# Keys and rotary queries turned by VectorE and DMA instead of TensorE, in the second sweep of a hybrid encoder layer

## The chip, the cores and the metric

The kernel runs on one core of a Trainium2 chip. The metric is the device time of one execution in microseconds (us); the median of several runs is given. Every stage works in float32, and most products are made of three matmuls on operands split into a high and a low part (names ending in `_h` and `_l`).

## The reference

One layer of an encoder over 2048 tokens of width 1024. One input projection feeds two groups: a gated linear attention with four heads, scanned forward and backward (group A), and a latent attention with four heads (group B). The outputs are joined, projected, and added to the residual with a layer norm. What the change touches is group B:

```python
def mla_branch(c_q, c_kv, k_rope, gate, positions, q_norm_g, w_uq, kv_norm_g, w_ukv):
    q = (rms_norm(c_q, q_norm_g) @ w_uq).reshape(B, S, 4, 128 + 64)
    kv = (rms_norm(c_kv, kv_norm_g) @ w_ukv).reshape(B, S, 4, 128 + 128)
    q_nope, q_rope = q[..., :128] * scale, apply_rope(q[..., 128:], positions) * scale
    k_nope, v = kv[..., :128], kv[..., 128:]
    k_r = apply_rope(k_rope, positions)
    ...   # for each block of 128 queries, over all 2048 keys:
    s = einsum('bqhd,bkhd->bhqk', qn, k_nope) + einsum('bqhr,bkr->bhqk', qr, k_r)
    o = einsum('bhqk,bkhv->bqhv', softmax(s), v)
    return o * silu(gate)
```

The kernel absorbs the key part of `w_ukv` into the queries, so that the normed latent `c_kv` (width 128) serves as key and as value for all heads, beside the rotary key of width 64.

## The kernel before

The tokens lie in 16 chunks of 128. The kernel has four stages one after the other.

1. **First sweep** (to about 338 us, with `late_gates` to about 349): group A's projections and scans, chunk by chunk in `sweep_a`. Its pieces are the functions `ga_...`. For most chunks, queries and keys are turned (tokens from partitions to columns) by VectorE's 32x32 stream transpose, four stores to DRAM and two loads (`turn`, `turned`). `ga_q` and `ga_k` make `qd` and `kd`, queries and keys with their decay; `ga_kt` turns `kd`.
2. **Second sweep** (`sweep_c`, 349 to about 583 us): 8 steps of two chunks. A step computes for its 256 tokens the gate of group B (`pz`, 96 matmuls in 8 parts), and for each chunk the projection `ipm` in four parts (`ipa` to `ipd`), from it the normed latents `cq` and `ckv` and the rotary key (`krf`, `krs`), the values `vh` and `vl`, and group A's last products `Ob` with its norm and gate (`oib`, `sqO`, `ss`, `rg...`, `og`, `oT`). `tm` turns `cq` (two transposes), `ckv` and `krs` (one each) on TensorE into PSUM, from which ScalarE and VectorE take `cqT_h/l`, `ckvT_h/l` and the turned `krs`. `pqr` projects the rotary queries, `qrf` rotates them, `tq` turns them by two transposes on TensorE, `qrTh/qrTl` split them, and `c_sqr` stores them (`rh_s`, `rl_s`). `pq` makes the absorbed queries `qah/qal`, stored by `c_sqa`.
3. **Attention** (to about 1080 us): 16 blocks of one head and 512 queries, each against all keys. `fetch(i)` loads the queries of block `i` into the buffers that held `pz`'s weights (`wz`); blocks 0 and 1 are fetched ahead of the loop.
4. **Output projection**, norm and store.

The order of all work in the second sweep is written by hand. `PLACE_C` gives each piece a place (step number plus a fraction, one for each chunk of the step where there are two); `PLACE_C_FIRST` and `PLACE_C_LAST` replace it in the first and the last step. `sweep_c` sorts all pieces by place and issues them in that order, and `in_order` chains the instructions of each engine, so that no engine overtakes:

```python
for _, _, fn, a in sorted(todo, key=lambda e: e[:2]):
    with self.in_order(last):
        fn(*a)
```

Nearly all DMAs are issued by SyncE (SP) from one queue in program order: a DMA that waits for its data or its buffer holds up those behind it. These are the loads of a chunk (`xcf`, the input; `SU`, `qdb`, `oib`, `ub`, group A's intermediate results) and the stores (`oa_s` from `oT`, `gm_s`, `qh_s`, `ql_s`, `rh_s`, `rl_s`). Matmul outputs lie in PSUM buffers of the tags `gp` (`pz`, `pq`, `Ob`), `ip` and `tr` (`tm`, `tq`, `pqr`).

Of the kernel before, what the change touches and what calls it, by code (L numbers as in the profile page):

```python
# [18 lines left out]
P = 128  # L19
# [4 lines left out]
H = 4  # L24
# [112 lines left out]
    "krsh", "krsl", "vh", "vl", "tm", "cqTh", "cqTl", "ckvTh", "ckvTl", "krT", "pqr", "qrf", "qrfa",  # L137
# [3 lines left out]
FETCH_C = ("lx", "xh", "xl")  # L141


PLACE_C = dict(
    ipa=(-0.08, 0.695),
# [6 lines left out]
    tq=(1.06, 1.482),  # L152
# [12 lines left out]
    qrTh=(1.16, 1.587),  # L165
# [11 lines left out]
    qrTl=(1.25, 1.687),  # L177
# [40 lines left out]
PLACE_C_FIRST = dict(  # L218
    ipa=(-1.874, 0.381),
# [6 lines left out]
    tq=(1.11, 1.512),  # L226
# [56 lines left out]
    Ob=(0.0, 0.299),  # L283
    tm=(0.495, 1.083),
    pqr=(0.749, 1.284),
    tq=(0.919, 2.161),
    xh=(-0.262, -0.109),
    sqO=(0.15, 0.374),
# [12 lines left out]
    oib=(0.063, 0.366),  # L301
# [23 lines left out]
    soT=(1.09, 2.304),  # L325
# [21 lines left out]
class K:  # L347
    def __init__(self, tc, ins, out):
        self.tc, self.nc, self.ins, self.out = tc, tc.nc, ins, out
        self.ulate = []  # L350
        self.parts = {}
# [141 lines left out]
    def run(self):  # L493
        tc, nc, ins = self.tc, self.nc, self.ins
        with ExitStack() as top:
# [8 lines left out]
            self.qr_s = [[dp.tile([H, 64, QB], F32, name=f"r{p}_s{b}") for p in "hl"] for b in range(NQB)]  # L504
            self.gm_s = [dp.tile([P, H, QB], F32, name=f"gm_s{b}") for b in range(NQB)]
            self.oa_s = [dp.tile([P, H, P], F32, name=f"oa_s{c}") for c in range(NCH)]
# [106 lines left out]
    def sweep_a(self):  # L613
        tc, nc, ins, cp = self.tc, self.nc, self.ins, self.cp
        with ExitStack() as ctx:
# [135 lines left out]
            run("k", i)  # L751
            run("q", i)
# [11 lines left out]
    def products(self, d, g, after=lambda g, k: None):  # L764
# [366 lines left out]
    def sweep_c(self):  # L1131


        with ExitStack() as ctx:
# [9 lines left out]
            def put(n, st, fn, *a, j=None):  # L1144
                last = st == len(steps) - 1
                p = PLACE_C[n]
                p = (last and PLACE_C_LAST.get(n)) or (not st and PLACE_C_FIRST.get(n)) or p
                todo.append((st + (p if j is None else p[j]), len(todo), fn, a))
# [3 lines left out]
            for s in steps:  # L1152
                for n in range(8):
                    put("pz", s["st"], self.c_pz, s, n, j=n)
                for n in STEP_C:
                    put(n, s["st"], getattr(self, "c_" + n), s)
            for d in chunks:
                for n in range(4):
                    put("ip" + "abcd"[n], d["st"], self.c_ip, d, n, j=d["j"])
                for n in CHUNK_C:  # L1160
                    if (d["st"] or n not in FETCH_C) and (d["c"] < NCH - 1 or n not in ("Sf1", "Sf2")):
                        put(n, d["st"], getattr(self, "c_" + n), d, j=d["j"])
            last = dict(self.tail)
# [42 lines left out]
    def scale_w(self, ct):  # L1206
        wa = self.w1.tile([P, H, P], F32, tag=f"qrT{'hl'[ct]}", name=f"wabs{ct}")
# [75 lines left out]
    def c_sqr(self, s):  # L1283
        b, qs = self.of_step(s)
        for t, dst in zip(s["qrT"], self.qr_s[b]):
            for pr in range(2):
                self.nc.sync.dma_start(dst[2 * pr:2 * pr + 2, :, qs].rearrange("h d t -> (h d) t"),
                                       t[:, pr].rearrange("p a t -> p (a t)").bitcast(F32))
# [57 lines left out]
    def c_krsh(self, d):  # L1346
        d["krs"] = self.w1.tile([P, 2, 64], F32R, tag="krs", name=f"krs{d['c']}")
# [10 lines left out]

    def c_tm(self, d):
        tp = d["tm"] = self.tr.tile([P, 4, P], F32, tag="tr", name=f"tm{d['c']}")  # L1360
        for i, src in enumerate((d["cq"][:, 0:P], d["cq"][:, P:2 * P], d["ckv"],
                                 d["krs"].rearrange("p a d -> p (a d)").bitcast(F32))):
            self.nc.tensor.transpose(tp[:, i], src, self.ident)
# [36 lines left out]
    def c_tq(self, d):  # L1400
        tq = d["tq"] = self.tr.tile([P, 4, P], F32, tag="tr", name=f"tq{d['c']}")
        for pr in range(2):
            self.nc.tensor.transpose(tq[:, pr], d["qr"][:, 2 * pr:2 * pr + 2].rearrange("p h d -> p (h d)"), self.ident)

    def c_qrTh(self, d):
        s = d["step"]
        if "qrT" not in s:
            s["qrT"] = [self.w1.tile([P, 2, 2, P], F32R, tag=f"qrT{p}", name=f"qrT{p}{d['st']}") for p in "hl"]
        self.hi(s["qrT"][0][:, :, d["j"]], d["tq"][:, 0:2])

    def c_qrTl(self, d):
        qrT, j = d["step"]["qrT"], d["j"]
        self.lo(qrT[1][:, :, j], d["tq"][:, 0:2], qrT[0][:, :, j])
# [106 lines left out]

    def attention(self):
# [4 lines left out]
        with ExitStack() as ctx:  # L1526
# [10 lines left out]
            def fetch(i):  # L1537
                h, b = blocks[i]
                q = stt[i]["q"] = []
                for p, src in zip("hl", self.qa_s[b]):  # L1540
                    q.append(qp.tile([P, QB], F32R, tag="wz", name=f"q{p}{i}"))
                    nc.sync.dma_start(q[-1].bitcast(F32), src[:, h])
                for p, src in zip("hl", self.qr_s[b]):
                    q.append(qp.tile([P, QB], F32R, tag="wz", name=f"r{p}{i}"))
                    for r in (slice(0, 64), slice(64, 128)):
                        nc.sync.dma_start(q[-1][r].bitcast(F32), src[h])

            def scores(i, j):
# [3 lines left out]
                qh, ql, rh, rl = d["q"]  # L1552
# [162 lines left out]
            fetch(0)  # L1715
            fetch(1)
# [22 lines left out]
            for i in range(nb):  # L1739
# [10 lines left out]
                if i + 2 < nb:  # L1750
                    put(NP * i + 4.05, fetch, i + 2)
# [300 lines left out]
```

## Time and profile before

| | |
|---|---|
| median of three runs | 1272.35 us (1271.3 to 1274.25) |
| the profiled execution | 1272.24 us, span 1270.3 us, mean granted clock 0.998 |
| TensorE, VectorE, ScalarE, GpSimd busy | 98%, 71%, 57%, 57% of the span |
| second sweep | some 349 to 583 us, steps of some 28.5 us |

The profile is of one execution. Its times count from the start of the span. PE is TensorE's matmul, PEld its weight load, DVE VectorE, ACT ScalarE, POOL GpSimd, SP SyncE with its DMA queue (SPq). A row of the timeline or the chain begins with start and duration; in brackets stands the idle time of the engine before it and what ended that. A row of a group has the line of the code, the engine, the operation, output and input tiles with shapes, the count, busy time, mean ns of one, and idle time before.

### The profile page before, as it was taken

Reading aid. Unit: us, or ns where it says so; the run is one execution under the profiler, and the core shown is the slowest. Engines: PE = TensorE matmul, PEld = TensorE weight load, DVE = VectorE, ACT = ScalarE, POOL = GpSimd, SP = SyncE. Lnnn points to the kernel's source line nnn. Section 1 sums busy time; section 2 is a strip of 40 time slices with the busy share of each in tenths; the row PEclk is TensorE's granted clock in tenths of the full one; section 3 lists DMA queues with packets and bytes.
Section 4 is the critical chain, followed back from the end, with each engine's and each line's share of the span. In section 5 each row is a group of like instructions: output and inputs, shape, how many; then the busy total and the mean of one; then the engine's idle time right before and its main releaser. Section 6 shows DMA issues by size and latency. Waiting matters only on the chain.

```text
span 1270.3 us, 19649 instructions
## 1 busy us (share of the span) xinstructions
PE 1246.8 (98%) x6946; PEld 1098.9 (87%) x6946; DVE 896.3 (71%) x1611; ACT 727.5 (57%) x1176; POOL 718.9 (57%) x443
## 2 busy tenths in 40 slices
PE   8999999999999999999999999999999999999997
PEld 7999999999799999988788888888888888887886
DVE  6635555553665555564888888888888888389997
ACT  7544343454565445454778888888888888411110
POOL 0132323223265555430798888889999999935541
PEclk9999999999999999999999999999999999999999
DMA  8224656566857766757212111201133110376652
GB/s 293 79 81 125 136 143 139 143 134 159 276 178 201 218 198 193 215 144 210 53 30 53 40 46 42 59 9 59 58 92 92 42 42 26 124 226 200 205 191 100
DMA packets 189794, 160.49 MB, mean 126 GB/s; under 512 B 98326, under 2 KB 140958, under 8 KB 189696
## 3 DMA queue, kind: packets, MB, share of 16 engines
q1 hardware_dynamic: 181632, 157.11, 43.4%
q0 software_dynamic: 672, 2.10, 0.4%
q8 instruction: 55, 0.90, 0.3%
q10 hardware_dynamic: 7392, 0.03, 0.3%
q14 instruction: 43, 0.35, 0.1%
HBM read 103.05 MB, written 56.13 MB: 125 GB/s over the span
## 4 chain that ended last, share of the span: by engine, by line
PE 68%; DVE 2%; ACT 1%; DMA 1%; issue 1%; POOL 0%; SPq 0%; DVEq 0%; POOLq 0%; ACTq 0%
PE pz L1239 7%; PE ipm L1310 5%; PE o L411 5%; PE o L413 5%; PE o L412 5%; PE pS L1556 4%; PE pS L1557 4%; PE pS L1558 4%; PE pS L1559 4%; PE pS L1560 4%; PE po L413 2%; PE po L411 2%; PE po L412 2%; PE Ob L1457 1%; PE pmb L413 1%
## 5 line engine op out<-in xcount | busy, mean ns | idle before, releaser
L363 POOL TENSOR_TENSOR pl<-s,ph 128x1024 fp32r<-128x1024 f32 x128 | 306.7, 2414 | 53.3 <-ACT ph L357 49.5
L1578 DVE TENSOR_TENSOR rm<-pS,rm 128x512 f32<-128x512 f32 x210 | 144.8, 690 | 36.4 <-ACT s L1565 30.8
L1565 ACT ACTIVATE s<-pS 128x1024 f32<-128x1024 f32 x128 | 131.3, 1025 | 61.2 <-PE pS L1560 50.8
L1602 DVE TENSOR_TENSOR s<-s,mb 128x1024 f32<-128x1024 f32 x128 | 151.2, 1213 | 8.9 <-PE mb L1596 8.2
L357 ACT ACTIVATE ph<-s 128x1024 fp32r<-128x1024 f32 x128 | 135.0, 1056 | 17.2 <-PE o L413 16.7
L1606 ACT ACTIVATE s<-s 128x1024 f32<-128x1024 f32 x128 | 131.4, 1049 | 10.6 <-DVE s L1602 10.5
L411 PE MATMUL ipa<-wah,xah 128*128 128x384 f32 (+1 forms) x384 | 129.1, 336 | 5.3 <-ACT wah L357 5.3
L412 PE MATMUL ipa<-wal,xah 128*128 128x384 f32 (+1 forms) x384 | 124.8, 325 | 0.0
L413 PE MATMUL ipa<-wah,xal 128*128 128x384 f32 (+1 forms) x384 | 124.7, 325 | 0.0
L1076 POOL TENSOR_TENSOR Sb<-Sb,Us 64x512 f32<-64x512 f32 x15 | 19.9, 1325 | 170.1 <-DVE Us L1068 161.0
L1556 PE MATMUL pS<-qh,ckvT_h 128*128 128x512 f32 x256 | 102.6, 401 | 0.8 <-DVE rm L1578 0.4
L411 PE MATMUL o<-ph,vh 128*128 128x512 f32 x256 | 101.1, 395 | 0.0
L1557 PE MATMUL pS<-ql,ckvT_h 128*128 128x512 f32 x256 | 100.0, 391 | 0.0
L1559 PE MATMUL pS<-rh,krs 128*128 128x512 f32 x256 | 100.0, 390 | 0.0
L1558 PE MATMUL pS<-qh,ckvT_l 128*128 128x512 f32 x256 | 99.9, 390 | 0.0
L1560 PE MATMUL pS<-rl,krs 128*128 128x512 f32 x256 | 99.8, 390 | 0.0
L413 PE MATMUL o<-ph,vl 128*128 128x512 f32 x256 | 99.8, 390 | 0.0
L412 PE MATMUL o<-pl,vh 128*128 128x512 f32 x256 | 99.7, 389 | 0.0
L1629 DVE TENSOR_TENSOR ap<-ap,s 128x512 f32<-128x512 f32 x120 | 83.0, 692 | 2.7 <-ACT s L1606 0.7
L411 PEld LDWEIGHTS ipa<-wah,xah 128*128 128x128 f32 x384 | 73.2, 191 | 8.5 <-ACT wah L357 5.6
L363 POOL TENSOR_TENSOR ol<-of,oh 128x512 fp32r<-128x512 f32 x32 | 43.0, 1345 | 64.6 <-ACT oh L357 63.1
L412 PEld LDWEIGHTS ipa<-wal,xah 128*128 128x128 f32 x384 | 73.2, 191 | 1.0 <-DVE wal L363 0.4
(302 smaller groups left out, 3426.0 us busy)
## 6 DMA issues: line engine op xcount, KB each, us to landing
xcf<-xT_dram SPq DMA_DIRECT2D x16, 512.0 KB, 5.6
xr<-x_dram SPq DMA_DIRECT2D x16, 512.0 KB, 6.6
out_dram<-rr SPq DMA_DIRECT2D x32, 256.0 KB, 2.1
xaf<-xT_dram SPq DMA_DIRECT2D x14, 512.0 KB, 4.2
oib<-oi_s SPq DMA_DIRECT2D x16, 256.0 KB, 4.4
qdb<-qd_s SPq DMA_DIRECT2D x16, 256.0 KB, 3.3
SU<-su_s SPq DMA_DIRECT2D x16, 256.0 KB, 3.7
ub<-u_s SPq DMA_DIRECT2D x16, 256.0 KB, 3.9
```

Source lines behind the costliest of these rows:

```text
L357: return nc.scalar.activation(dst, src, AF.Copy).ins
L363: return e.tensor_tensor(dst, src, hi.bitcast(F32), ALU.subtract).ins
L411: mm(out, ah, bh, start=start, stop=False)
L412: mm(out, ah, bl, start=False, stop=False)
L413: mm(out, al, bh, start=False, stop=stop)
L1556: mm(ps[:, e], kh, qh, start=True, stop=False)
L1557: mm(ps[:, e], kh, ql, start=False, stop=False)
L1558: mm(ps[:, e], kl, qh, start=False, stop=False)
L1559: mm(ps[:, e], kr, rh, start=False, stop=False)
L1560: mm(ps[:, e], kr, rl, start=False, stop=True)
L1578: V.tensor_tensor(d["rm"], src[:, e], d["rm"], ALU.max)
L1602: V.tensor_tensor(s, s, d["mb"][:, None, :].to_broadcast([P, 2, QB]), ALU.subtract)
```

## The change

- For chunks 0 to 13, `ckv` and `krs` are no longer turned by `tm`. A new piece `kvx` turns `vh`, `vl` and `krs` of a chunk in 32x32 blocks on VectorE (three stream transposes), `skv` stores a step's result in four DMAs to DRAM (`kv_s`), and `kv_load` loads it back, in four DMAs, into one tile `kvT` that takes the place of `ckvT_h`, `ckvT_l` and the turned `krs`. The two chunks of the last step keep the transposes on TensorE.
- `tq` becomes one stream transpose of 128x256 on VectorE into SBUF (`qrx`); `qrTh/qrTl` read that; `c_sqr` stores in eight DMAs (runs of 128 bytes) instead of four; `fetch` reads each block's rotary queries in eight DMAs of 32 partitions instead of four of 64.
- `fetch` of blocks 0 and 1 becomes part of the second sweep's order (places 8.23 and 9.35), ahead of the last stores; the rotary queries' store of step 6 and the `oT` stores of chunk 14 get later places.
- In the last step chunk 15's `Ob` (with `oib` and `sqO`) goes from place 0.299 to 0.425, which on TensorE is from behind chunk 13's `tm` to just ahead of step 6's `pq`, and `tq`, `qrTh`, `qrTl` get slightly other places.
- The last chunk of the first sweep turns its keys by four TensorE transposes and a copy instead of stream transpose, stores and loads, and `kd` is made ahead of `qd`.
- As a result of the issue order, `qal` of the last step comes on VectorE behind block 0's first maxima, just ahead of `mc`.

The core of the diff (the remaining hunks shift places of pieces named above by a few hundredths):

```diff
+LAST_C = ("ckvTh", "ckvTl", "krT")
+KV_LOADS = tuple((2 * s - 4, 2 * s - 2, float(s)) for s in range(2, NCH // 2)) + ((12, 14, 8.27),)
+LATE_STORE = {("sqr", 6): 2.31}
 PLACE_C = dict(
+    skv=1.65,
+    kvx=(1.02, 1.44),
...
-    tq=(1.06, 1.482),
+    tq=(1.13, 1.56),
 PLACE_C_LAST = dict(
...
-    Ob=(0.0, 0.299),
+    Ob=(0.0, 0.425),
...
-    soT=(1.09, 2.304),
+    soT=(1.29, 2.304),
@@ run
-            self.ckvT_h = rp.tile([P, NKT, P], F32R, name="ckvT_h")
-            self.ckvT_l = rp.tile([P, NKT, P], F32R, name="ckvT_l")
-            self.kr = rp.tile([P, NKT, P], F32R, name="krs")
+            self.kvT = rp.tile([P, NKT, 3, P], F32R, name="kvT")
+            self.ckvT_h, self.ckvT_l, self.kr = (self.kvT[:, :, i] for i in range(3))
@@ sweep_a
-            run("k", i)
-            run("q", i)
+            with self.in_order(last):
+                run("k", i)
+                run("q", i)
@@ products
-            for n in ((("lr", "qx"), ("ql", "kx", "v1"), ("kl", "v3")) if i else (("lr",), ("q2", "k2", "v1"), ("v3",)))[g]:
+            for n in ((("lr", "qx"), ("ql", "k2", "v1"), ("v3",)) if i == NCH - 1 else
+                      (("lr", "qx"), ("ql", "kx", "v1"), ("kl", "v3")) if i else (("lr",), ("q2", "k2", "v1"), ("v3",)))[g]:
@@ sweep_c
+            for a, b, place in KV_LOADS:
+                todo.append((place, len(todo), self.kv_load, (slice(a, b),)))
+            for i, place in enumerate((8.23, 9.35)):
+                todo.append((place, len(todo), self.fetch, (i,)))
@@ c_sqr
-        for t, dst in zip(s["qrT"], self.qr_s[b]):
-            for pr in range(2):
-                self.nc.sync.dma_start(dst[2 * pr:2 * pr + 2, :, qs].rearrange("h d t -> (h d) t"),
-                                       t[:, pr].rearrange("p a t -> p (a t)").bitcast(F32))
+        dst = self.qr_s[b].rearrange("r p h a (c e t) -> e r (p h a) c t", c=4, e=4)
+        for j in range(2):
+            t = s["qrT"][:, j].rearrange("p a (m t) -> p (a m) t", t=32).bitcast(F32)
+            for e in range(4):
+                self.nc.sync.dma_start(dst[e, :, :, qs.start // P + j], t[32 * e:32 * e + 32])
+    def c_kvx(self, d):
+        s = d["step"]
+        if "kvx" not in s:
+            s["kvx"] = self.w1.tile([P, 2, 3, P], F32, tag="kvx", name=f"kvx{d['st']}")
+        for i, src in enumerate((self.vh[:, d["c"]], self.vl[:, d["c"]], d["krs"].rearrange("p a d -> p (a d)"))):
+            self.nc.vector.transpose(s["kvx"][:, d["j"], i], src.bitcast(F32))
+    def c_skv(self, s):
+        t = s["kvx"].rearrange("p a i (m t) -> p (a i m) t", m=4)
+        c = 2 * s["st"]
+        dst = self.kv_s[:, c:c + 2].rearrange("r a i m (b t) -> b r (a i m) t", b=4)
+        for b in range(4):
+            self.nc.sync.dma_start(dst[b], t[32 * b:32 * b + 32])
+    def kv_load(self, cs):
+        for m in range(4):
+            self.nc.sync.dma_start(self.kvT[32 * m:32 * m + 32, cs].rearrange("p c i t -> p (c i) t").bitcast(F32),
+                                   self.kv_s[:, cs, :, m].rearrange("r c i t -> r (c i) t"))
@@ c_tm
-        for i, src in enumerate((d["cq"][:, 0:P], d["cq"][:, P:2 * P], d["ckv"],
-                                 d["krs"].rearrange("p a d -> p (a d)").bitcast(F32))):
-            self.nc.tensor.transpose(tp[:, i], src, self.ident)
+        src = (d["cq"][:, 0:P], d["cq"][:, P:2 * P])
+        if d["st"] == NCH // 2 - 1:
+            src += d["ckv"], d["krs"].rearrange("p a d -> p (a d)").bitcast(F32)
+        for i, e in enumerate(src):
+            self.nc.tensor.transpose(tp[:, i], e, self.ident)
@@ c_tq
-        tq = d["tq"] = self.tr.tile([P, 4, P], F32, tag="tr", name=f"tq{d['c']}")
-        for pr in range(2):
-            self.nc.tensor.transpose(tq[:, pr], d["qr"][:, 2 * pr:2 * pr + 2].rearrange("p h d -> p (h d)"), self.ident)
+        d["tq"] = self.w1.tile([P, 256], F32, tag="qrx", name=f"qrx{d['c']}")
+        self.nc.vector.transpose(d["tq"], d["qr"].rearrange("p h d -> p (h d)"))
@@ fetch (a method now)
+        for n, p in enumerate("hl"):
+            q.append(qp.tile([P, QB], F32R, tag="wz", name=f"r{p}{i}"))
+            for r in range(4):
+                nc.sync.dma_start(q[-1][32 * r:32 * r + 32].bitcast(F32), self.qr_s[b][:, n, h, r % 2])
@@ attention
-            fetch(0)
-            fetch(1)
```

More of the change, by code (lines that the diff above doesn't have):

```diff
@@ L218 @@
 PLACE_C_FIRST = dict(
+    skv=1.66,
+    kvx=(0.95, 1.5),
     ipa=(-1.874, 0.381),
@@ L1146, in put @@
                 p = PLACE_C[n]
-                p = (last and PLACE_C_LAST.get(n)) or (not st and PLACE_C_FIRST.get(n)) or p
+                p = (last and PLACE_C_LAST.get(n)) or (not st and PLACE_C_FIRST.get(n)) or LATE_STORE.get((n, st)) or p
                 todo.append((st + (p if j is None else p[j]), len(todo), fn, a))
```

56 lines of the change are left out of this document (31 added, 25 removed).

## The prediction

> **What bounds the kernel now.** I read the page first: its engine totals and the chain that ended last.
>
> ```profile
> span 1270.3 us, 19649 instructions
> PE 1246.8 (98%) x6946; PEld 1098.9 (87%) x6946; DVE 896.3 (71%) x1611; ACT 727.5 (57%) x1176; POOL 718.9 (57%) x443
> PE 68%; DVE 2%; ACT 1%; DMA 1%; issue 1%; POOL 0%; SPq 0%; DVEq 0%; POOLq 0%; ACTq 0%
> ```
>
> TensorE (PE) is idle for 23.5 us of the span, and the chain runs along it. Work taken off PE is time, as long as nothing else becomes late. Where that can happen is told by the table of busy time by stage (first the stretch, its length and PE's busy time; later DVE, ACT, POOL, clock, DMA share, GB/s), over the end of the first sweep, one step of the second sweep, its last step in two parts, and the start of attention.
>
> ```profile
> 320.00:338.00 18.00, 15.78 (x102) 13.47 (x101) 11.92 (x18) 7.37 (x15) 7.49 (x9) 1.00 0.75 241
> 338.00:349.00 11.00, 11.00 (x54) 9.22 (x53) 8.10 (x13) 9.34 (x17) 1.68 (x3) 1.00 1.04 381
> 448.00:477.00 29.00, 29.00 (x215) 28.26 (x214) 15.48 (x56) 14.56 (x41) 14.59 (x17) 1.00 0.71 200
> 534.00:566.00 32.00, 29.24 (x190) 26.73 (x190) 18.01 (x65) 16.37 (x46) 9.25 (x11) 1.00 0.56 149
> 590.00:620.00 30.00, 27.17 (x121) 21.49 (x120) 24.39 (x31) 19.62 (x22) 7.39 (x4) 1.00 0.65 179
> ```
>
> In a middle step PE never stops, DVE is half idle, and the DMA engines are 71% busy. So the second sweep up to about 534 us is bound by PE alone. In the last step (from 534) PE already waits 2.8 us, and 2.8 us again at the start of attention. The clock is granted in full throughout, so it plays no part.
>
> **The transposes taken off PE.** The chain of waits shows what one costs there.
>
> ```profile
> 536.50 0.44 PE tm L1363 x4
> 536.93 2.88 PE pz L1239 x24
> 574.87 0.22 PE tq L1403 x2
> ```
>
> Four in 0.44 us and two in 0.22: 0.11 us each in PE's stream. Removed are 2 of every chunk's 4 `tm` for 14 chunks (28) and all `tq` (32): 60 x 0.11 = 6.6 us at most. By my count 50 of them lie ahead of chunk 13's `Ob`, where PE is never idle; 6 lie in the stretch of the last step where PE waits anyway (below), and 4 are the `tq` of the two last chunks. I count 54 x 0.11 = 5.9 us. [...]
>
> **What DVE gets.** The change adds three 128x128 stream transposes a chunk (`kvx`) and one of 128x256 (`qrx`), and takes away one `ckvT_l`. The nearest rows are:
>
> ```profile
> L814 DVE STREAM_TRANSPOSE qx<-ipa 128x256 f32<-128x256 f32 x1 | 0.4, 440 | 0.0
> L1486 DVE STREAM_TRANSPOSE oT<-og 128x512 f32<-128x512 f32 x16 | 11.4, 711 | 0.5
> L363 DVE TENSOR_TENSOR ckvT_l<-tm,ckvT_h 128x128 fp32r<-128x128 f32 x16 | 4.6, 285 | 12.0 <-ACT ckvT_h L357 12.0
> ```
>
> A line through 440 and 711 gives 0.30 for 128 columns (bounds 0.18, a quarter of 711, and 0.44). A step of two chunks then gets 2 x (0.9 + 0.44 - 0.28) = 2.1 us: DVE 17.6 of some 28, still no bound by its total. But it works in order, and one place has little room: `og` of the second chunk frees a PSUM buffer that the next step's first `pz` writes.
>
> ```profile
> 464.78 1.13 DVE L1480 SCALAR_TENSOR_TENSOR og<-Ob,rg_r,ub 128x128 f32<-128x128 f32 x4
> 466.80 0.37 PE L1239 MATMUL pz<-xch,wzh 128*128 128x256 f32 x1
> ```
>
> `og` ends at 465.91, 0.9 us ahead of `pz`. PE will be there 0.44 earlier (two `tq`, two `tm`), and three `kvx` (0.9) come ahead of this `og` on DVE, of which DVE's short waits for ACT inside that chain swallow some half. So 0 to 0.4 us a step is lost, at most 2.4 in six steps; I take 0.1 a step, 0.6. ACT loses two copies a chunk and has only less to do.
>
> **What the queue and the DMA engines get.** Per step four stores `kv_s`, four loads `kvT` and four more stores of rotary queries are added, all on SyncE's queue, which issues in order.
>
> ```profile
> L1492 SPq DMA_DIRECT2D oa_s<-oT x52: 573/630/1139, 404.4 to 574.2; - x52
> SPq L1418 <- PE Ob L1457: 54.6, 9, 10.6
> 451.48 1.13 SPq L477 DMA_DIRECT2D xcf<-xT_dram  x1
> 460.83 1.05 ACT L357 ACTIVATE xch<-xcf 128x1024 fp32r<-128x1024 f32 x1
> xcf<-xT_dram SPq DMA_DIRECT2D x2, 512.0 KB, 5.6
> ```
>
> `oa_s` has the form of the new stores, 512 runs of 128 bytes: 0.63 us of issue. Twelve more are 7.6 us a step, and SyncE sits some 55 us of the sweep in its waits for `Ob` alone, about 7 a step; it becomes full, but not over-full. Most exposed is `xcf`, which comes behind the four `kv_s`: issued at 451.48, landed 5.6 later at 457.1, needed by ACT at 460.83, 3.7 us of room; 0.44 goes to the earlier PE and 4 x 0.63 = 2.5 to the stores, which leaves 0.8. I count nothing; the price if the cover goes is a rival below. What the added packets cost the DMA engines is bounded by two stretches:
>
> ```profile
> DMA packets 7828, 5.81 MB, mean 200 GB/s; under 512 B 4496, under 2 KB 6544, under 8 KB 7824
> DMA packets 2155, 4.19 MB, mean 381 GB/s; under 512 B 414, under 2 KB 542, under 8 KB 2155
> ```
>
> The second (338 to 349, DMA share 1.04) moves a megabyte in 11 x 16 x 1.04 / 4.19 = 43.7 us of engine time. At that price the bytes of the first (448 to 477) explain 254 of its 0.71 x 16 x 29 = 329 us; the other 75, over 4,496 packets under 512 B, are 17 ns a packet. A step gets 7,168 more such packets in place of 512 of a kilobyte, 768 of 512 bytes, and 0.79 MB more: by bytes alone 34 us (share 0.78), with 17 ns on each of 7,400 net 160 us, which is 1.05. I take the middle, 0.92: no wait on PE.
>
> **The end of the first sweep.** The last chunk's keys no longer go to DRAM and back, `kd` runs ahead of `qd`, and PE gets four transposes.
>
> ```profile
> 328.72 1.40 DVE L991 SCALAR_TENSOR_TENSOR qd<-q,E 128x512 f32<-128x512 f32 x1 [1.10 <-ACT E L974]
> 330.04 2.04 DVE L1005 TENSOR_TENSOR kd<-k,E 128x512 f32<-128x512 f32 x1
> 332.13 0.66 PE L1027 MATMUL kt<-ident,kd 128*128 128x128 f32 x4 [1.65 <-DVE kd L1005]
> ```
>
> `kd` started at 328.72 ends by 330.8 even at its 2.04 us, so PE's 1.65 us goes; the four new transposes cost 0.44 to 0.66. Gain 1.0 (bounds 0, if `qd` is now what PE waits for, and 1.2).
>
> **The last step, where I see the loss.** `oib` of chunk 14 is already the last thing DVE waits for, and behind it on DVE stands everything up to the second half of `pz`.
>
> ```profile
> 546.29 0.32 SPq L1418 DMA_DIRECT2D qdb<-qd_s  x1
> 547.18 0.86 SPq L1287 DMA_DIRECT2D rh_s<-qrTh  x2
> 548.13 0.97 SPq L1287 DMA_DIRECT2D rl_s<-qrTl  x2
> 549.15 0.92 SPq L1418 DMA_DIRECT2D oib<-oi_s  x2
> 553.52 0.70 DVE L1460 TENSOR_TENSOR Ob<-Ob,oib 128x512 f32<-128x512 f32 x1 [3.82 <-DMA oib<-oi_s]
> 566.70 0.71 DVE L1486 STREAM_TRANSPOSE oT<-og 128x512 f32<-128x512 f32 x1
> 566.72 4.56 PE pz L1239 x36
> ```
>
> The list of waits has, for the same stretch, PE's longest one:
>
> ```profile
> PE Ob L1457 <- DVE og L1480: 2.1, 1, 2.1
> ```
>
> `qdb` waits for PE's `Ob` of chunk 13, so all behind it is tied to PE. After it come four stores (1.97 us) and `oib`; in the changed order eight stores stand there, 8 x 0.63 = 5.0 us, so `oib` lands 3.1 us later. From 553.5 to 566.7 DVE works almost without a gap, and gets in this stretch three `kvx` of chunk 13 (0.9) and one `qrx` (0.44), less one `ckvT_l` (0.28): `pz` starts 3.1 + 1.1 = 4.2 us later against `Ob` 13. Bounds: 0, if the stores are issued while SyncE would have waited anyway, and 5.3 with `kvx` at 0.44 and the load slower among the stores. Moving `Ob` 15 further back on PE spares PE these 2.1 us there, but that only moves the wait, since `pz` needs the same DVE chain. I take 4.2.
>
> **The start of attention.**
>
> ```profile
> 578.49 0.54 SPq L1542 DMA_DIRECT2D qh<-qh_s  x1
> 602.69 0.39 PE L1556 MATMUL pS<-qh,ckvT_h 128*128 128x512 f32 x1
> 605.25 0.66 PE L1584 MATMUL mx<-ident,rm 128*128 128x128 f32 x4 [1.27 <-DVE rm L1578]
> 605.95 0.69 DVE L1589 TENSOR_REDUCE mc<-mx 128x4 f32<-128x512 f32 x1 [0.75 <-PE mx L1584]
> 567.34 1.19 DVE L363 TENSOR_TENSOR qal<-pq,qah 128x1024 fp32r<-128x1024 f32 x1
> ```
>
> The last `qal` now runs just ahead of `mc`: 1.19 us where DVE had 0.75 free, so block 0's maximum comes 0.45 later, with PE waiting. I add 0.25 for the loads: 0.7 (bounds 0 and 3). The second block's queries stand behind four `kvT`, eight stores of `oT`, eight of rotary queries and `gm`: with their own ten, 31 issues of 0.6 behind the first block's, some 18.6 us. From about 581 that is 599.6, and with 5 to land 604.6; the first use is at 602.69, plus the 4.2 that PE is late by then. So it just holds.
>
> **Sum:** against the profiled execution's 1272.24 (0.1 under the median of the runs): -5.9 -1.0 +0.6 +4.2 +0.7 = -1.4, so 1270.8 us. Its own range is 1268 to 1273. About 0.2%, 2.5 us, is what a measurement of this kernel tells from no change, so the forecast lies within that, near its edge.
>
> **Rival 1, the last step absorbs it.** If the eight stores go out under SyncE's wait, or the DVE chain has slack that the waits do not show, the 4.2 goes and the 6 transposes there count: 1270.8 - 4.2 - 0.7 = 1265.9; the second block's queries, then 1.9 us late, take some back: 1266 to 1268. For it speaks that PE's 2.1 us for `og` stand ahead of `Ob` 15, whose move avoids them; against it that `oib` is the releaser now.
>
> **Rival 2, slower: `xcf` late in every step.** Its cover of 0.8 us means that it may take 6.4 us to land. In the crowded stretch 320 to 338, at a DMA share of 0.75, it took
>
> ```profile
> xcf<-xT_dram SPq DMA_DIRECT2D x1, 512.0 KB, 9.3
> ```
>
> At 9.3 each of six steps loses 2.9; halfway, 7.9, it loses 1.5: 6 x 1.5 = 9, so 1279.8. It decides from 6.4 us on. For it speaks the DMA share going to 0.92; against it that at 0.71 the load takes 5.6.
>
> **Rival 3, small packets saturate the DMA engines.** At the upper bound of 1.05 a step lasts 29 x 1.05 = 30.5 us instead of PE's 29 - 0.9 = 28.1: six steps lose 14, so 1285. [...]
>
> **Rival 4, the change doesn't shorten PE:** each step's stall takes the transposes' place and only the 1.0 and the last step's loss remain: 1274 to 1276.
>
> **Chances.** Forecast 0.43, rival 1 0.30, rival 2 0.15, rival 3 0.05, rival 4 0.07. Below 1269.8 lie rival 1 and about two fifths of the forecast: 0.47. Above 1274.9 lie rivals 2 and 3, half of 4 and a little of the forecast: 0.25. The rest, 0.28, is within. The range leaves out one in ten at each end: 1265 to 1279.
>
> **What will show it.** Right: in a middle step PE still 100% busy and the step 0.8 to 0.9 us shorter; DVE's wait for `oib` in the last step near 7 us and `pz`'s second half some 2 us earlier than before by the clock; `kd`'s wait gone. Wrong: PE waits for `xch`, `xcl` or `og` in every step (rivals 2 to 4), or no longer wait for `oib` (rival 1).

## The result and the profile after

The changed kernel takes 1285.86 us (median of four runs, 1283.77 to 1287.85) against 1271.82 for the kernel before: 1.0108 times as long, 95% interval 1.0083 to 1.0133. The forecast was 1270.8, with 1265 to 1279 as its range. The kernel is slower by 14 us, more than any case but the third rival had priced, and for other reasons than that rival's.

The page of the changed kernel, and its table of busy time by stage:

```profile
span 1282.0 us, 19691 instructions
PE 1245.0 (97%) x6890; PEld 1095.9 (85%) x6890; DVE 908.8 (71%) x1654; ACT 725.8 (57%) x1149; POOL 720.4 (56%) x443
```
```profile
320.00:338.00 18.00, 17.42 (x119) 15.31 (x118) 10.32 (x18) 8.40 (x18) 8.21 (x11) 1.00 0.72 235
448.00:477.00 29.00, 28.14 (x205) 27.20 (x203) 18.18 (x62) 14.18 (x38) 14.55 (x16) 1.00 0.92 226
534.00:566.00 32.00, 25.46 (x148) 23.25 (x147) 16.33 (x59) 13.77 (x37) 13.36 (x17) 0.90 0.87 201
600.00:630.00 30.00, 19.91 (x83) 15.68 (x82) 17.55 (x22) 14.52 (x17) 4.93 (x3) 0.89 0.77 197
```

The end of the first sweep is fuller than before (17.42 of 18 against 15.78). In the middle steps PE now waits, 0.9 us of the 29 shown and 1.9 in the next 29 (477 to 506). In the last step it is idle 6.5 us of 32, at the start of attention 10 of 30, and in both the granted clock is no longer 1.00 (0.90 and 0.89). The list of PE's waits between 300 and 640 us names them:

```profile
PE pS L1600 <- DVE rm L1622: 8.7, 1, 8.7
PE pz L1260 <- DVE og L1523: 4.7, 6, 1.6
PE pqr L419 <- ACT cqT_h L365: 4.5, 1, 4.5
PE ipm L1332 <- ACT ckv L1359: 1.2, 1, 1.2
PE mb L1640 <- DVE mc L1633: 1.1, 1, 1.1
PE pqr L421 <- DVE cqT_l L371: 0.9, 1, 0.9
```

Where the time went is seen best by the start of the same matmul in both timelines (us from the span's start; the difference in the last column):

| first matmul of | before | after | after - before |
|---|---|---|---|
| `ipm` of chunk 0 (second sweep begins) | 348.86 | 347.81 | -1.05 |
| `Ob` of chunk 13 (middle steps done) | 545.21 | 545.26 | +0.05 |
| second half of the last `pz` | 566.72 | 571.91 | +5.19 |
| block 0's first score | 583.30 | 588.16 | +4.86 |
| block 1's fifth score tile | 615.25 | 628.70 | +13.44 |
| the last block's maxima (`mx`) | 1065.76 | 1079.09 | +13.33 |

So: 1.05 gained at the end of the first sweep; in the middle steps not only nothing kept of 5.5 us of transposes taken off PE, but 1.1 lost besides; 5.1 lost in the last step; 8.5 lost behind block 0's scores. After that the two run alike. The output stage is some 1.7 us shorter than in the profile of before, but it is shorter in every later profile too, by 0.3 to 1.6 us, also in that where only the first sweep differs; I take it for that one execution's.

### The profile page after: what moved, and what is told of

Same layout as the page of the kernel before. It is cut to its first block, busy times and chain, and to the rows that moved or that the text cites. A ratio compares the mean times of both kernels' runs of the same rounds, so it can differ in the third digit from the quotient of the medians.

```text
span 1282.0 us, 19691 instructions
## 1 busy us (share of the span) xinstructions
PE 1245.0 (97%) x6890; PEld 1095.9 (85%) x6890; DVE 908.8 (71%) x1654; ACT 725.8 (57%) x1149; POOL 720.4 (56%) x443
## 4 chain that ended last, share of the span: by engine, by line
PE 80%; DMA 5%; DVE 4%; issue 3%; POOL 3%; SPq 3%; ACT 2%; DVEq 0%; POOLq 0%; ACTq 0%
PE pz L1260 6%; PE o L419 4%; PE o L420 4%; PE o L421 4%; PE pS L1600 4%; PE pS L1601 4%; PE pS L1602 4%; PE pS L1603 4%; PE pS L1604 4%; PE ipa L419 4%; PE ipa L421 4%; PE ipa L420 4%; PE ipg L421 2%; PE ipg L419 2%; PE ipg L420 2%
## 5 line engine op out<-in xcount | busy, mean ns | idle before, releaser
L1600 PE MATMUL pS<-qh,kvT 128*128 128x512 f32 x256 | 102.9, 402 | 8.7 <-DVE rm L1622 8.7
L1601 PE MATMUL pS<-ql,kvT 128*128 128x512 f32 x256 | 100.4, 392 | 0.0
L1602 PE MATMUL pS<-qh,kvT 128*128 128x512 f32 x256 | 100.2, 391 | 0.0
L1603 PE MATMUL pS<-rh,kvT 128*128 128x512 f32 x256 | 100.1, 391 | 0.0
L1604 PE MATMUL pS<-rl,kvT 128*128 128x512 f32 x256 | 100.0, 391 | 0.0
L1260 PE MATMUL pz<-xch,wzh 128*128 128x256 f32 x256 | 72.8, 288 | 4.7 <-DVE og L1523 4.7
```

The lines of the kernel that those rows point to most:

```text
L1260: self.nc.tensor.matmul(s["pz"][:, h], self.Wz[k][w][:, h * P:(h + 1) * P], x2(x, k), start=(k == 0 and p == 0), stop=stop.get(h) == (k, p))
L1600: mm(ps[:, e], kh, qh, start=True, stop=False)
L1601: mm(ps[:, e], kh, ql, start=False, stop=False)
L1602: mm(ps[:, e], kl, qh, start=False, stop=False)
L1603: mm(ps[:, e], kr, rh, start=False, stop=False)
L1604: mm(ps[:, e], kr, rl, start=False, stop=True)
```

## The experiments

All times are ratios to the kernel before, run beside each kernel on the same chip. "Middle steps" is the change of `Ob` 13's start from before, less that of chunk 0's `ipm`: 5.5 us earlier is the full saving; the changed kernel is at +1.1. It is read from one profiled execution each, and it varies: experiments 1 and 3, whose middle steps are the changed kernel's, are at +0.1 and +0.35. Differences of about 1 us in it show nothing by themselves.

**1. The load of wvf.** Behind block 0's scores ScalarE's queue stands, waiting for a DMA; the timelines of ScalarE and SyncE of the changed kernel, and SyncE's row of the kernel before:

```profile
614.30 0.37 SPq L1760 DMA_DIRECT2D wvf<-wv_dram  x1
620.06 0.72 ACT L1763 ACTIVATE wvf<-wvf,gkv_c 128x512 f32<-128x512 f32 x1 [10.22 <-DMA wvf<-wv_dram]
```
```profile
L1718 SPq DMA_DIRECT2D wvf<-wv_dram x1: 530/530/530, 595.4 to 595.4; - x1
```

Before, the load was issued 12.1 us behind block 0's first score and landed 0.6 us before ScalarE used it; now it is issued 26.1 us behind: 38 DMAs stand between the two instead of 14, among them the whole fetch of block 1 and 25 stores instead of 11. The edit puts the load right behind block 0's fetch (and its tile into another buffer):

```diff
+            todo.append((8.24, len(todo), self.wv_load, ()))   # a wz buffer, right behind fetch(0)
...
-            nc.sync.dma_start(wv, self.ins["wv"])
+            wv = self.wv
```

> The changed kernel with one DMA moved: the load of wvf (values' weights) goes onto SyncE's queue right behind the first block's queries instead of behind the last qal store. Theory A (the 9.3 us lost after block 0's scores are ScalarE waiting for wvf, whose load stands on SyncE behind the ql store, which waits for the late qal): PE's wait of 8.7 us at the scores of block 1 goes, the slow clock behind it too, and the time falls by 8 to 9.5 us, to about 1277. Rival B (PE there waits for the second block's queries or for saturated DMA engines): the wait stays above 5 us and the time stays above 1282. Nothing changes ahead of attention under either: block 0's first scores stay some 4.8 us later than in the kernel before.

Measured 1.0013 (1.0004 to 1.0022), 1274.39 us: 9.5 thousandths, 12 us, off by the ratios. PE's 8.7 us wait is gone and block 1's scores keep their distance (+4.23 at block 0, +3.50 at block 1). Theory A holds, but one link in it was wrong: in the changed kernel SyncE did not wait for `qal`, which ended at 610.16, 0.6 us before its store was issued. SyncE issued without a pause from 604.5 to 611.4; the load was late by the mere length of the queue ahead of it.

**2. kvx behind og.** VectorE's timeline of the changed kernel in a middle step, where `rm_r` ends one norm and `rg_t` goes on with `og`'s:

```profile
463.34 0.16 DVE L441 TENSOR_TENSOR rm_r<-rm_t,ipm 128x2 f32<-128x2 f32 x1
463.51 0.31 DVE L1387 STREAM_TRANSPOSE kvx<-vh 128x128 f32<-128x128 f32 x1
463.75 0.27 DVE L1387 STREAM_TRANSPOSE kvx<-vl 128x128 f32<-128x128 f32 x1
463.94 0.27 DVE L1387 STREAM_TRANSPOSE kvx<-krs 128x128 f32<-128x128 f32 x1
464.14 0.12 DVE L438 TENSOR_TENSOR rg_t<-Ob,ss 128x4 f32<-128x4 f32 x1
464.89 1.13 DVE L1523 SCALAR_TENSOR_TENSOR og<-Ob,rg_r,ub 128x128 f32<-128x128 f32 x4
```

```diff
-    kvx=(1.02, 1.44),      # first step (0.95, 1.5)
+    kvx=(1.105, 1.44),     # first step (1.174, 1.5)
```

> The changed kernel with the first chunk's three kvx transposes of each step placed behind og and oT on VectorE instead of ahead of og's norm. Theory A (in every middle step the saved transposes are given back because these 0.8 us of VectorE stand ahead of og, which frees the PSUM buffer of the next pz): PE's waits for og in the middle steps (4.7 us in 6 waits) fall below 1.5, chunk 13's Ob comes 4 to 6 us earlier than in the changed kernel, and the time falls by about as much, to 1280 to 1282. Rival B (DMA engines or SyncE's queue, 85 to 93% busy in these steps, hold the steps): chunk 13's Ob moves by less than 1.5 us and the time stays within 2 us of the changed kernel's.

Measured 1.0073 (1.0058 to 1.0088), 3.5 thousandths better. Middle steps -2.1 instead of +1.1; PE's waits for `og` fell from 4.7 to 1.7 us. So the place matters. How much of the 6.6 us missing it explains is less certain: 3.2 between these two profiles, but only 2.2 against experiment 1's, and experiments 4 and 5 with the same place are at +0.5 and -1.6. Over 3 us remained.

**3. oib ahead of the stores.**

```diff
-LATE_STORE = {("sqr", 6): 2.31}
+LATE_STORE = {("sqr", 5): 1.88, ("sqr", 6): 2.31}
```

> The changed kernel with the load of oib of chunk 14 ahead of the eight rotary-query stores of step 5 instead of behind them. Theory A (the last step's 5.2 us are that load coming late, with VectorE's queue behind it, and PE running at a lower clock after its idle 4.5 us): oib lands some 5 us earlier relative to Ob of chunk 13, PE's 4.5 us at pqr go, the second half of pz starts 4 to 5 us earlier, and the time falls to 1281 to 1282. Rival B (VectorE's added transposes set the chain, or the loads are slow among many packets): the second half of pz moves by less than 2 us.

Measured 1.0079 (1.0062 to 1.0095), 2.9 thousandths better. From `Ob` 13 to the second half of `pz` the loss against before falls from 5.1 to 3.5 us: 1.6 us of the 4 to 5 that theory A said, and less than the 2 us that rival B allowed. The load was only one part. PE's wait of 4.5 is down to 1.5, but new ones came (1.5 for `og`, 1.1 for `cqT_l`).

**4. All three.**

> All three moves together on the changed kernel. Theory A (three separate places): the gains add, 9 + 5 + 4.5 = 18.5 us off, to about 1267, some 4 us below the kernel before. Rival B (the places hang together, or SyncE's full queue makes the next load late): less than 13 us off, 1273 or more, not faster than the kernel before.

Measured 0.9981 (0.9971 to 0.9991), 1270.42 us: 12.7 thousandths, 16 us, off the changed kernel. One by one the three came to 15.9 thousandths, 20 us, and theory A had 18.5 us; given the intervals this does not tell whether the gains add in full. Rival B falls; still, it is only just faster than the kernel before. What made the changed kernel slower than the one before lies in these three places, then, and what the transposes should have saved is still missing. In its profile the middle steps gave everything back (+0.5). A part of that is PE's clock, which was at half from 496.7 for 3.4 us (see the last section).

**5. ub ahead as well.** With `oib` in time, VectorE's `og` of chunk 14 waited 3.24 us for `ub`, which stands behind the same stores.

```diff
-("sqr", 5): 1.88        # and the key loads of place 7.0
+("sqr", 5): 2.31        # key loads at 7.32
```

> The three moves together, and the eight rotary-query stores of step 5 and the four key loads of place 7 also behind the load of ub of chunk 14. In the three moves together VectorE's og of chunk 14 still waited 3.24 us for that ub, which stood behind these twelve DMAs on SyncE. Theory A (what the last step still loses, some 3.2 us between Ob of chunk 13 and the second half of pz, is this place in the queue): the wait goes, pz's second half starts 2 to 3.5 us earlier against Ob 13, and the time falls from 0.998 of the kernel before to about 0.9955. Rival B (VectorE's added transposes set that chain): less than 1 us.

Measured 1.0 (0.9987 to 1.0013): no gain. The wait for `ub` of chunk 14 went, but the loss between `Ob` 13 and `pz` grew from 3.2 to 4.9. The wait had only moved on: the eight stores and four loads now stand ahead of `ub` of chunk 15, which is issued at 565.75, and VectorE waits for that.

```profile
569.24 1.13 DVE L1528 SCALAR_TENSOR_TENSOR og<-Ob,rg_r,ub 128x128 f32<-128x128 f32 x4 [2.67 <-DMA ub<-u_s]
```

PE's second half of `pz` starts behind this `og`, at 570.42. So neither theory had it: the queue decided, at its next load.

**6. Key loads in two batches.**

```diff
-KV_LOADS = ... (2 * s - 4, 2 * s - 2, float(s)) for s in range(2, 7) ...
+KV_LOADS = ((0, 6, 4.0), (6, 12, 7.32), (12, 14, 8.27))
```

> As the run with ub ahead, and the key loads of the middle steps in two batches (chunks 0 to 5 at place 4, 6 to 11 in the last step) instead of five: twelve DMAs fewer on SyncE in the middle, the same bytes. Theory A (SyncE's full queue makes the ql stores land late, for which ScalarE's first pass over pz waits 2 to 2.6 us in middle steps): the steps without key loads have that wait shortened by up to 1.8 us, Ob of chunk 13 comes 1 to 3 us earlier against the start of the second sweep than with ub ahead alone, and the time is 0.993 to 0.995 of the kernel before. Rival B (the middle steps lose nothing more once kvx stands behind og): no more than 0.5 us.

Measured 1.0039 (1.0025 to 1.0053), slower. The steps without key loads gain nothing over experiment 5 (-1.2 at chunk 7 against -1.6), in the one with the batch PE waits 2.2 us at once, and the second batch lengthens the last step. Bursts of loads were no cure here.

**7. Key stores doubled.**

```diff
+            for _ in range(2):
                 self.nc.sync.dma_start(dst[b], t[32 * b:32 * b + 32])
```

> The three moves together, with each of the four key stores of a step issued twice (the same bytes to the same place): four more DMAs of 768 packets a step, 2.6 us more of SyncE's time and 2.5 us more of 16 DMA engines. Nothing else differs. Theory A (queue and DMA engines are full in the middle steps): each of seven steps lengthens by 1 to 2.5 us, 7 to 17 us in all, 1277 to 1288. Rival B (there is room): within 2 us of the three moves together.

Measured 1.0513 (1.0497 to 1.0529): 9.6 us for each step, far beyond either theory. SyncE's waits in its middle steps tell why:

```profile
SPq L1400 <- DMA kv_s<-kvx: 35.7, 16, 4.7
```

The second store of a pair goes to the same place and waits for the first to land, 2.2 us each time. So it lengthened above all the queue's time, by some 10 us a step, and PE's step grew by nearly all of it. It shows that the queue has no room for that; how much it had left, and whether the queue or the DMA engines were full, it does not tell.

**8. Keys on TensorE again, queries on VectorE.**

```diff
-                    late = d["st"] == len(steps) - 1
+                    late = True            # no kvx, skv, kv_load; tm with four transposes
```

> As the run with ub ahead, but the keys stay on TensorE in all steps, as in the kernel before (four transposes in tm, no kvx, no key stores or loads); only the rotary queries go by VectorE. Half of the saving in PE's stream (0.44 us a step, 3 us in all), with a third of the added DMAs. Theory A (queue full): no middle step gives anything back, Ob of chunk 13 comes 3 us earlier than in the kernel before counted from the start of the second sweep, and the time is 0.995 to 0.997 of before, no worse than with all keys turned. Rival B (the queue has room, VectorE's order was all): 3 us slower than the run with ub ahead.

Measured 0.996 (0.9946 to 0.9975), 1267.87 us: faster than before, and faster than experiment 5, from which it differs by the keys alone. The middle steps keep 2.3 of the 2.4 us that their 22 transposes are worth, and PE waits for nothing in them. SyncE's waits between 390 and 534 us (before, changed kernel, this one; two longest each):

```profile
SPq L1418 <- PE Ob L1457: 31.0, 6, 6.4
SPq L1281 <- ACT ckv L1337: 17.5, 4, 5.5
```
```profile
SPq L1302 <- DVE qal L371: 4.5, 3, 2.5
SPq L1310 <- DVE rope L1547: 4.1, 4, 1.4
```
```profile
SPq L1307 <- ACT ckv L1364: 21.7, 5, 5.4
SPq L1466 <- PE Ob L1505: 8.2, 6, 2.6
```

All rows of these lists together come to some 71 us before, 23 in the changed kernel and 53 with the queries alone. Before, SyncE mostly waits for engines, and its loads go out as soon as a buffer is free. In the changed kernel it runs behind, and engines wait for what it issues late.

**9. The key DMAs on ScalarE's queue.**

```diff
-            self.nc.sync.dma_start(dst[b], ...)         # kv_s, and kvT of chunks 0 to 11
+            self.nc.scalar.dma_start(dst[b], ...)
```

> As the run with ub ahead (all keys and rotary queries turned by VectorE), but the key stores and the key loads of chunks 0 to 11 are issued by ScalarE's queue instead of SyncE's: the same DMAs, bytes and transposes, eight issues a step fewer on SyncE. Theory A (the middle steps give their saving back because SyncE's queue, one DMA after the other, has become full): SyncE waits again for PE's Ob and ScalarE's ckv in the middle steps, Ob of chunk 13 comes 4 to 5.5 us earlier counted from the start of the second sweep instead of 1.6, minus what ScalarE loses to issuing (0.4 us each, up to 4 us a step of which it has over half idle). Rival B (the 16 DMA engines are the limit): no gain in the middle steps, since the same packets move.

Measured 1.0118 (1.0101 to 1.0136), 15 us for the worse of experiment 5. With the loads alone moved:

> As the run with ub ahead, with only the key loads of chunks 0 to 9 issued by ScalarE (four a step, 1.8 us less of SyncE's time); the stores stay on SyncE. Theory A (SyncE's queue full): Ob of chunk 13 1 to 3 us earlier, counted from the start of the second sweep, than with ub ahead. Rival B (DMA engines the limit): no change.

1.0053 (1.0032 to 1.0074), 7 us for the worse. Neither tells the theories apart: SyncE now waits for ScalarE's DMAs (the first of the two runs, between 390 and 534 us),

```profile
SPq L1540 <- DMA kvT<-kv_s: 16.1, 5, 3.7
SPq L1466 <- DMA kv_s<-kvx: 9.5, 2, 5.5
```

and those come when ScalarE reaches them. The two queues were coupled, not relieved. What couples them no run shows; on the one queue of the changed kernel, between 390 and 534 us, none of 137 DMAs was issued before the one eight places ahead of it had landed, and two of 136 were before the one seven ahead had (those for which the trace has that landing).

**10. Keys on VectorE, queries on TensorE.**

```diff
-        self.nc.vector.transpose(d["tq"], ...)     # tq, qrT, c_sqr, fetch as before the change
+            self.nc.tensor.transpose(tq[:, pr], ..., self.ident)
```

> As the run with ub ahead, but the rotary queries are turned on TensorE and stored in four DMAs as in the kernel before; only the keys go by VectorE and DMA. The other half of the saving (0.44 us a step) with eight added DMAs a step instead of four. Theory A (queue): the middle steps keep 0 to 0.3 us each, less than with the queries turned alone, and the time is 0.997 to 1.0 of the kernel before. Rival B (only VectorE's order counted): the middle steps keep 0.44 each, 0.996, the same as with the queries alone.

Measured 1.0094 (1.0075 to 1.0112). This came out badly for a reason of its own: the queries' buffer is single again, its store of step 6 stands behind the first fetch as in the changed kernel, and ScalarE waits for it; PE is idle for 9.5 us ahead of the last `tm`. What remains usable is the middle steps: -0.2 of 3 us. There PE waited three times for GpSimd's `qrf` (1.5 us), as `tq` has the place of the kernel before, so it doesn't settle the theories either.

**11. Long runs.** The same DMAs and bytes in runs of 3 KB. This kernel leaves out the exchange of the 32x32 blocks between partitions, so its keys of chunks 0 to 13 are in the wrong order; its work is otherwise the same.

```diff
-        dst = self.kv_s[:, c:c + 2].rearrange("r a i m (b t) -> b r (a i m) t", b=4)
+            self.nc.sync.dma_start(self.kv_s[r, s["st"]], t[r])      # plain rows; kvT likewise
```

> As the run with ub ahead, but the key stores and loads move plain rows: four stores and four loads a step as there, the same bytes, in runs of 3 KB (32 packets of 3 KB a DMA) instead of 768 runs of 128 bytes and 192 of 512. Left out is the exchange of the 32x32 blocks between partitions, so the keys of chunks 0 to 13 are in the wrong order. Theory A (short runs: they lengthen each issue on SyncE from about 0.4 to 0.63 us and keep the DMA engines at 85 to 93%): Ob of chunk 13 comes 4 to 5.5 us earlier counted from the start of the second sweep, against 1.6 with ub ahead, and the time is 0.994 to 0.997 of the kernel before. Rival B (the number of DMAs on the one queue, or VectorE's added transposes): no more than 1 us better than with ub ahead, 0.999 to 1.0.

Measured 0.9948 (0.9933 to 0.9963), 5.2 thousandths better than experiment 5, from which it differs in nothing else. The middle steps keep 3.9 us instead of 1.6. The two kernels' rows for the key stores in the middle steps (nanoseconds to issue, min/median/max; first experiment 5), and two stretches of the busy table, again 5 first:

```profile
L1399 SPq DMA_DIRECT2D kv_s<-kvx x20: 328/769/1361, 390.6 to 512.1; - x20
448.00:477.00 29.00, 28.63 (x207) 27.62 (x206) 17.33 (x62) 14.43 (x39) 14.87 (x17) 1.00 0.90 225
477.00:506.00 29.00, 27.75 (x198) 26.55 (x197) 17.88 (x62) 13.09 (x36) 15.98 (x18) 1.00 0.95 228
```
```profile
L1398 SPq DMA_DIRECT2D kv_s<-kvx x18: 421/444/1424, 389.7 to 507.2; - x18
448.00:477.00 29.00, 29.00 (x214) 28.30 (x213) 18.24 (x63) 14.39 (x38) 16.92 (x18) 1.00 0.90 241
477.00:506.00 29.00, 28.61 (x207) 27.60 (x206) 17.38 (x62) 13.73 (x36) 15.35 (x17) 1.00 0.91 236
```

The DMA engines are as busy as ever, 0.90 and 0.91, and PE all but never waits: a DMA share of 0.9 alone did not slow these steps. VectorE has the same transposes. Each store is issued faster, by 0.33 us in the median but by only 0.16 in the mean (0.77 to 0.61), 0.6 us of SyncE's time a step. SyncE's list of waits has not become longer: 23 us in all, as in the changed kernel, against 30 in experiment 5. So of the three suspects it is the short runs. Whether they cost by their time on the issuing queue or by the delay of the packets themselves stays open.

**12. The end of the first sweep alone.**

```diff
+            with self.in_order(last):          # on the kernel before: kd ahead of qd,
+                run("k", i); run("q", i)       # and the last chunk's keys turned on TensorE
```

> The kernel before with one part of the change alone: the last chunk's keys of the first sweep turned on TensorE, and kd ahead of qd. Theory A: PE's 1.65 us wait for kd goes for four transposes, 1.0 us off, 0.9992 of the kernel before, at the edge of what 5 rounds tell. Rival B (qd becomes late instead): no change or slower.

Measured 0.9979 (0.997 to 0.9988), 1269.59 us against 1272.55: faster by 2.7 us (1.5 to 3.8). PE's wait for `kd` is gone from its list of waits. By the starts of matmuls 1.8 us are gained there and 1.4 are left at the end, so the interval's lower end is the better figure.

**13. The best version.** Experiment 8 with chunk 15's `Ob` back at its old place and step 6's rotary-query store behind the second fetch:

```diff
-    Ob=(0.0, 0.425),   # oib 0.43, sqO 0.435
+    Ob=(0.0, 0.299),   # oib 0.366, sqO 0.374
-LATE_STORE = {..., ("sqr", 6): 2.31}
+LATE_STORE = {..., ("sqr", 6): 3.4}
```

> The run with keys on TensorE and queries turned by VectorE, with two more moves: Ob, oib and sqO of chunk 15 back at the places of the kernel before (TensorE had waited some 2.5 us around it), and the rotary-query stores of step 6 behind the second block's query loads, so that gm's store and with it qal come earlier. Theory A (each is one wait on the path): up to 2 us off, 0.9945 to 0.9955 of the kernel before. Rival B (the waits only move): within 0.5 us of the run with keys on TensorE, 0.996.

Measured 0.9951 (0.9931 to 0.997), 1266.32 us: 6 us faster than the kernel before, and faster than experiment 8 by about what theory A said, though the intervals overlap. The second half of `pz` starts 4.2 us earlier than before, against 2.1 in experiment 8, so the move of `Ob` 15 was itself a loss.

## Why the prediction was wrong

- **First sweep's end, right in the wait, uncertain in size.** PE's wait for `kd` went. Forecast -1.0 with 1.2 as the bound; measured -1.05 at the start of the second sweep, and by itself 2.7 us off the whole time, with 1.5 as the lower end. That the one number fits so well has luck in it: over the later profiles with the same first sweep this start lies between -1.8 and +0.4.
- **60 transposes at 0.11 us, right in price, wrong in what is kept.** Where nothing else became late (experiment 8) they brought 2.3 of 2.4 us. The step that failed is the cover: "0 to 0.4 us a step is lost ... I take 0.1". The three `kvx` last 0.31 + 0.27 + 0.27, near the 0.9 estimated, and since each starts before the last one ends they hold `rg_t` up by 0.63. But I let ScalarE's waits swallow half of that, and the rows of `rm_r` to `rg_t` show none there to swallow it. Moving them brought 4.5 us by the ratios, whose intervals just overlap.
- **SyncE's queue: "it becomes full, but not over-full", wrong.** I priced 0.63 us a store from `oa_s`; with 768 runs `kv_s` took 0.77. Above all I asked only whether `xcf` still lands in time. What came late was something else: ScalarE's first pass over `pz` (`gm`) waits for the store of `ql` to land, whose buffer it writes; ScalarE's waits between 390 and 534 us of the changed kernel (total, times, longest):

```profile
ACT gm L1265 <- DMA ql_s<-qal: 3.3, 3, 2.0
ACT qrT L365 <- DMA kvT<-kv_s: 2.2, 2, 1.5
```

  Before, ScalarE waits for no DMA there, and with the queries alone for 0.2 us. The store itself is not held up in the queue; what is late is `SU`, a load that the change doesn't touch. One step of the kernel before, then the same step of the changed one:

```profile
470.02 1.29 POOL L1441 TENSOR_TENSOR Sf<-Sf,SU 64x512 f32<-64x512 f32 x1 [1.53 <-DMA SU<-su_s]
477.43 1.23 DVE L363 TENSOR_TENSOR qal<-pq,qah 128x1024 fp32r<-128x1024 f32 x1 [3.68 <-ACT qah L357]
```
```profile
470.01 0.57 SPq L1461 DMA_DIRECT2D SU<-su_s  x1
474.12 1.28 POOL L1484 TENSOR_TENSOR Sf<-Sf,SU 64x512 f32<-64x512 f32 x1 [5.38 <-DMA SU<-su_s]
478.64 0.45 DVE L1446 STREAM_TRANSPOSE qrx<-qrf 128x256 f32<-128x256 f32 x1 [3.98 <-POOL qrf L1442]
479.01 1.19 DVE L371 TENSOR_TENSOR qal<-pq,qah 128x1024 fp32r<-128x1024 f32 x1
480.22 0.56 SPq L1302 DMA_DIRECT2D ql_s<-qal  x1
484.67 1.03 ACT L1265 ACTIVATE gm<-pz 128x1024 f32<-128x1024 f32 x1 [2.00 <-DMA ql_s<-qal]
```

  `SU` is issued 4.4 us later than before (465.65 there), behind four key loads and four more query stores. GpSimd waits for it and reaches `qrf` late; VectorE's new `qrx` waits for `qrf` and stands ahead of `qal`, which before came 0.04 us behind `qah` and now 2.3; its store is issued at once, but lands late for `gm`. VectorE's work up to `og` follows late, 0.63 of it for the three `kvx`, and PE waits 1.6 us for `og`. GpSimd's waits for `SU` between 390 and 534 us come to 5.1 us before, 23.6 in the changed kernel, 18.8 with long runs and 3.1 with the queries alone. This chain is read from the rows; no run moved `SU` by itself. The queue ran behind and delayed also what the change doesn't touch. That is fourth-rival territory ("each step's stall takes the transposes' place"), given a chance of 0.07.
- **Last step, right in place, near in size, partly by luck.** Forecast 4.2 later, measured 5.1 from `Ob` 13 on. The stores took 5.47 us for eight, and VectorE used the load 2.5 us later than before (forecast 3.1); its wait for it was 2.87 us, not near 7. From there to `pz` its chain took 2.7 us longer (forecast 1.1), 1.5 of them a wait for PE's `Ob` 15, which PE reached late and at half clock; that I left out (below). That the forecast tied `oib` alone to it was too simple, as experiments 3 and 5 show.
- **Start of attention: 0.7 forecast, 8.5 measured.** The step that failed is the list of what the moved loads go past. I followed the second block's queries through the queue and not `wvf`, which the change doesn't touch and which had 0.6 us to spare. This one omission is more than half of the error. The second block's queries, which I did follow, came in time as forecast: PE's first use of them, at 606.35, has no wait. (Before, that use was at 601.56; the row that I took for it, 602.69, is the second half of the same score tile.)
- **Third rival.** Its time (1285) is near the measured one, its mechanism is not: with 3 KB runs the DMA share stayed at 0.9 and most of the loss in the middle steps went. My own 0.92 for that share was met to the digit, by luck: it was the middle between 0.78 and 1.05. The length of the runs showed in the time (1.0 to 0.9948, experiments 5 and 11) and in the issue of the stores (0.77 to 0.61 us in the mean), and in the engines' share hardly (0.90 and 0.95 to 0.90 and 0.91).

## What to carry to other kernels

When a step is moved ahead on an in-order queue, list every transfer that it passes and the time each has to spare, those that the change doesn't name first: here `wvf`, with 0.6 us to spare, cost PE a wait of 8.7 us. Work moved off the bounding engine onto a chain that frees its buffers can come back as a wait, and belongs behind the last instruction of that chain: PE's waits for `og` were 4.7 us with `kvx` ahead of it and 1.7 with it behind. When a DMA queue's waits for engines shrink (here from 71 to 23 us), look for the loads that now land late (GpSimd's waits for `SU` went from 5.1 to 23.6 us), also on engines off the path, and follow what stands behind them in each engine's order; the DMA share told nothing of it here, at 0.9 with 3 KB runs as with the short ones.

## What was not expected of the hardware

PE's waits cost more than their length here. After its idle 4.47 us in the last step, and after 8.71 behind block 0's scores, the same matmuls come at half the rate. PE's timeline of the changed kernel, two neighbouring `ipm` ahead of the first wait and two behind it, then the second wait:

```profile
553.59 0.36 PE L1332 MATMUL ipm<-wml,xch 128*128 128x448 f32 x1
553.79 0.36 PE L1332 MATMUL ipm<-wmh,xch 128*128 128x448 f32 x1
...
560.68 0.58 PE L419 MATMUL pqr<-wqr_h,cqT_h 128*128 128x256 f32 x1 [4.47 <-ACT cqT_h L365]
...
563.72 0.57 PE L1332 MATMUL ipm<-wml,xch 128*128 128x448 f32 x1
564.10 0.57 PE L1332 MATMUL ipm<-wmh,xch 128*128 128x448 f32 x1
...
624.75 0.77 PE L1600 MATMUL pS<-qh,kvT 128*128 128x512 f32 x1 [8.71 <-DVE rm L1622]
```

The pitch goes from 0.20 to 0.38 us. The granted clock is 0.50 from 559.9 to 566.7, and PE is busy for 5.2 us of that: about 2.6 us more lost. Behind the second wait the scores come every 0.43 us instead of 0.23 until 628.1, 1.6 us more; the granted clock is 0.50 from 621.3. So the clock fell 3.7 us into the first wait and 5.3 us into the second. The 2.07 us wait of the kernel before had no such tail: the granted clock of its last step is 1.00. Other runs show the half clock behind shorter waits. In experiment 11 no wait of PE in the last step is over 1.5 us; two stretches of its table (length and PE's busy time first, the clock third from the end):

```profile
548.60:552.00 3.40, 1.64 (x8) 1.01 (x6) 3.26 (x17) 1.45 (x7) 0.27 (x1) 1.00 1.00 214
552.00:558.80 6.80, 5.95 (x23) 5.65 (x24) 4.64 (x17) 0.52 (x3) 3.98 (x5) 0.50 0.60 115
```

PE was idle for 1.8 of 3.4 us, in pieces, and then ran at half clock for 6.8. One wait's length did not decide here: behind one of 2.04 us in experiment 12 the clock was at half for 3.4 us, behind the 2.07 of the kernel before not at all. The forecast, which held that the clock plays no part, left this price out.

DMAs issued from a second engine's queue did not relieve the first: in experiment 9 SyncE spent 16.1 us in five waits for ScalarE's loads, and ScalarE 17.0 us in five that ended with a key store's landing.
